# An encoder trunk with expert retrieval: gather indices copied on VectorE, sparse steps from the fourth tile, smaller last dumps

## The chip, the cores and the metric

The kernel runs on one core of one Trainium2 chip. The metric is the device time of one execution in microseconds (us). Three runs of the kernel before took 1835.06 us in the median, 1828.98 at the least and 1835.87 at the most. The engines are called TensorE (PE, with PEld for its weight loads), VectorE (DVE), ScalarE (ACT), GpSimd (POOL) and SyncE (SP). SP here only issues the loads of weights; POOL issues the gathers.

## The reference

Two layers over 272 tokens (256 and 16 meta tokens) of width 1024. Layer 0 mixes tokens with a recurrent block, layer 1 with a convolution; behind each mixer stands the same retrieval of experts (PEER):

```
q = (xc @ w_query)                             # 8 heads, two halves
s1, i1 = top_k(scores[:, :, 0], 16); s2, i2 = top_k(scores[:, :, 1], 16)
cand = s1[..., :, None] + s2[..., None, :];  s, flat = top_k(cand, 16)
expert = idx1 * 128 + idx2                     # one of 16384 experts
g = softmax(s)
act = gelu(einsum('chkd,cd->chk', expert_u[expert], xc))
out = einsum('chk,chkd->cd', g * act, expert_v[expert])
```

Each token and head picks 16 of 16384 experts; an expert's row of U gives an activation, its row of V is added with that weight. Everything is float32.

## The kernel before

**Dense passes.** For most tokens the kernel does not gather experts. It multiplies all of them: the *U pass* computes the activations of all 128 x 128 experts for a block of tokens, one tile of 128 experts after another, weighs them by a one-hot product (`g_unit`), and the *V pass* multiplies them by all rows of V, again in 128 tiles. A tile of weights is loaded by SP into one of four buffers `raw` (`load`), split into a high and a low part (`load_split`, L137: `hi` on ScalarE L144, `lo` on VectorE or POOL L151) and multiplied. In the V pass a tile is eight products with `hi` (L718) and eight with `lo` (L722), which add up in PSUM. The activations are split the same way, four tiles at a time (`weights`, L260 and L263).

**Few tokens.** Tokens that don't fit the dense block are served sparsely, in groups of 16 tokens, where a partition is one head of one token. A group is *early*, *late* or *drawn*. In layer 1 one group is early (from token 240) and two are drawn (224 and 208); in layer 0 one is early, one late, none drawn. For early and late groups, rows of U are gathered by POOL (`few_rows`, L989) and multiplied on VectorE (`few_dot`, L998). A drawn group's activations exist already, as its tokens went through the dense U pass. They are dumped to a table in DRAM, and each of its 16 activations a partition is then fetched by one gather of one number a partition (`few_draw`, L1004). For all groups, rows of V are gathered by POOL and added up on VectorE (`few_add`, L1027 and L1029), with two rows asked for ahead.

**Dumps.** `few_dump` copies a piece of the activations to a tile `own` (L698, two buffers) and sends it to the table (L699), both on POOL. Before the change a piece is 32 of 128 rows; four pieces for each of two groups, the last ones behind the last tile of the U pass. The list `dumps` says behind which tile of the second half of U a piece goes.

**The order of the V pass.** `few_plan` makes a list of steps (load of `wide`, dots, activation, weighing, adds) and spreads them over the tiles of V: a step has a tile at which it is due. Draws get due tiles of their own, a dozen tiles or more into the pass. `few_step` runs behind each tile: it takes one piece of the pending top-k work (`picks`, the generator `few_late`: per drawn group nine pieces, then a softmax), then all steps that are due:

```
        with self.tc.issue_after(self.dve_lo.ins):
            while self.picks:
```

The block around it ties VectorE's instructions of this tile behind the tile's `lo`; instructions on other engines in the block are not tied. What runs when on POOL and SP is decided by a planner that orders the program by its own costs, by data and by buffers. The scratch of the picks and the rows lies in pools that are opened when the pool of `own` is closed.

Of the kernel before, what the change touches and what calls it, by code (L numbers as in the profile page):

```python
# [7 lines left out]
F32 = mybir.dt.float32  # L8
F32R = mybir.dt.float32r
F16 = mybir.dt.float16  # L10
U32 = mybir.dt.uint32
# [6 lines left out]
P = 128  # L18
# [6 lines left out]
TOPK = 16  # L25
NK = 128
# [7 lines left out]
FEW = META  # L34
# [2 lines left out]
DOTS_FROM, DOTS, AHEAD, LO_FROM = 48, 10, 2, 41  # L37
JG = 4
JA = 64
JD = 32  # L40
FULL = (("v", 1024),)
SQ_AT = 4
PE_TAPS = (0, 0, 0, 0, 0, 6, 31, 31)
# [18 lines left out]
class Trunk:  # L62
# [481 lines left out]
    def peer(self, layer, n, xs):  # L544
        tc, nc, a = self.tc, self.nc, self.a
# [9 lines left out]
        with tc.tile_pool(name=f"few{layer}", bufs=1) as kp:  # L555
# [3 lines left out]
            act_a = ap0.tile([P, JA, nu], F32, name="act_a")  # L559

            with tc.tile_pool(name=f"top{layer}", bufs=1) as sp:
# [7 lines left out]
                early, late = [], []  # L569
# [22 lines left out]
                drawn = [self.few_pick(sp, kp, q, xs, layer, t0) for t0 in DRAWN[layer]]  # L592
# [31 lines left out]
            with tc.tile_pool(name=f"act1{layer}", bufs=1) as ap1:  # L624
                act_b = ap1.tile([P, NK - JA, nu], F32, name="act_b")
# [3 lines left out]
                rp = drawn_pool.__enter__()  # L629
                dumps = {}  # L630
                for g, few in enumerate(drawn):
                    few["table"] = self.dp.tile([P, NK, FEW], F32, name=f"own{layer}_{few['t0']}")
                    for j in range(0, NK, JD):
                        dumps.setdefault(j + JD - 1 - JA if j >= JA else (g * JA + j) // JD * 8 + 3, []).append((few, j))

                def weigh(dst, g):
                    nc.vector.scalar_tensor_tensor(dst, g, scale, dst, op0=OP.mult, op1=OP.mult)  # L637
# [23 lines left out]
                def g_unit(c0, jd):  # L661
                    cs = slice(c0, c0 + CC)
                    one_hot(c0)
                    ps = self.px.tile([P, CC, NK], F32, tag=f"g{c0 // CC % 2}", name="g")
                    for c in range(CC):
                        A, Bh, Bl = hot.pop(c0 + c)
                        nc.tensor.matmul(ps[:, c, :], A, Bh, start=True, stop=False)  # L667
                        nc.tensor.matmul(ps[:, c, :], A, Bl, start=False, stop=True)  # L668
                    pj = ps.rearrange("p c j -> p j c")
                    weigh(act_a[:, :, cs], pj[:, :JA, :])  # L670
                    if jd > JA:
                        weigh(act_b[:, :jd - JA, cs], pj[:, JA:jd, :])
                    if jd < NK:
                        nc.scalar.activation(act_b[:, jd - JA:, cs], pj[:, jd:, :], AF.Copy, scale=scale)  # L674
# [4 lines left out]
                def u_out(i, ps):  # L679
                    cd = at[0] * CC  # L680
                    w = act_b[:, i, :]
                    if cd < nu:
                        nc.scalar.activation(w[:, cd:], ps[:, cd:], AF.Gelu_apprx_tanh)
                    if cd > 0:
                        tmp = hp.tile([P, n], F32, tag="tmp", name="tmp")
                        nc.scalar.activation(tmp[:, :cd], ps[:, :cd], AF.Gelu_apprx_tanh)
                        nc.vector.tensor_tensor(w[:, :cd], w[:, :cd], tmp[:, :cd], op=OP.mult)
                    for few, j in dumps.get(i, ()):
                        few_dump(few, j)
                    upto = min(len(chunks), (i + 1) * len(chunks) // (NK - JA - 4))  # L690
                    for c0 in chunks[at[0]:upto]:
                        g_unit(c0, JA + i + 1)
                    at[0] = upto

                def few_dump(few, j):
                    own = rp.tile([P, JD, FEW], F32, tag="own", name="own")
                    act, o = (act_a, j) if j < JA else (act_b, j - JA)
                    nc.gpsimd.tensor_copy(own, act[:, o:o + JD, few["t0"]:few["t0"] + FEW])  # L698
                    nc.gpsimd.dma_start(few["table"][:, j:j + JD], own)  # L699

                acc = []
                self.upper(f"gate{layer}")
                self.linears([U[j] for j in range(JA, NK)], xs, nu, (("v", 1024),), u_out)
                hot_pool.__exit__(None, None, None)
                drawn_pool.__exit__(None, None, None)
# [3 lines left out]
                vp = row_pool.__enter__()  # L709
# [291 lines left out]
            few["rows"][nxt] = self.few_rows(pool, few, self.a["u_rows"], 0, nxt, ahead + 1)  # L1001

    def few_draw(self, few, k):
        self.nc.gpsimd.indirect_dma_start(  # L1004
            out=few["act"][:, k:k + 1], out_offset=None, in_=few["table"].rearrange("p j (t o) -> (p j t) o", o=1),
            in_offset=bass.IndirectOffsetOnAxis(ap=few["ids"][:, 0, k:k + 1], axis=0))

    def few_gelu(self, few, last):
        self.nc.scalar.activation(few["act"], few["act"], AF.Gelu_apprx_tanh)
# [23 lines left out]
    def few_plan(self, vp, kp, early, late, drawn, scale, layer, ahead=2):  # L1033
        steps = []
        draws = []
        for few in early + late + drawn:
            lo = DOTS if few in early else 0
            if few["drawn"]:
                draws += [(len(steps), lambda few=few, k=k: self.few_draw(few, k)) for k in range(TOPK)]
            else:  # L1040
                steps += [lambda few=few: self.few_load(vp, few)]
                steps += [lambda few=few, lo=lo, k=k: self.few_dot(vp, few, k, lo, TOPK, ahead) for k in range(TOPK - lo + ahead)]
                steps += [lambda few=few: self.few_gelu(few, few is (early + late)[-1])]
            steps += [lambda few=few: self.few_weigh(few, scale)]
            steps += [lambda few=few, k=k: self.few_add(vp, few, k, ahead) for k in range(TOPK + ahead)] + [few]
        self.steps = [(1 + i * (NK - 4 * JG - 1) // len(steps), f) for i, f in enumerate(steps)]
        first = 12 * (len(late) + 1)
        for i, (at, f) in enumerate(draws):
            g, k = divmod(i, TOPK)
            lo, hi = first + 12 * g, self.steps[at][0] - 3  # L1050
            draws[i] = lo + k * (hi - lo) // TOPK, f
        self.steps = sorted(self.steps + draws, key=lambda s: s[0])
        self.sums = []
        self.picks = [self.few_late(kp, few, layer) for few in late + drawn]

    def few_step(self, j):
        with self.tc.issue_after(self.dve_lo.ins):
            while self.picks:
                try:
                    next(self.picks[0])  # L1060
                    break
                except StopIteration:
                    self.picks.pop(0)
            while self.steps and self.steps[0][0] <= j:
                f = self.steps.pop(0)[1]
                if callable(f):
                    f()
                else:
                    self.sums.append((j + 4, f))
        while self.sums and self.sums[0][0] <= j:  # L1070
            yield self.sums.pop(0)[1]
# [245 lines left out]
```

## Time and profile before

| what | before |
|---|---|
| median of three runs | 1835.06 us |
| the profiled execution, its own time | 1841.34 us |
| its span | 1839.5 us |
| TensorE busy (share of the span) | 1770.1 us (96%) |
| VectorE busy | 1508.1 us (82%) |
| ScalarE busy | 914.6 us (50%) |
| POOL busy | 473.8 us (26%) |
| mean DMA rate | 215 GB/s |

The span is the time from the first to the last instruction of the program in the profile. Times of rows are counted from its start. A row of a timeline has start, duration, engine, line, operation, tiles and shape, and in brackets how long the engine had been idle and what released it; `remote` and "another core or an unknown queue" stand for a releaser that the profile cannot name. Layer 1's U pass runs to about 1468 us, its V pass from there to the end.

### The profile page before, as it was taken

The numbers are of one execution on the slowest core, as the hardware profiler recorded it, in microseconds if no ns is written. First come the engines' busy times: TensorE is split into PE (matmuls) and PEld (weight loads), VectorE is DVE, ScalarE is ACT, GpSimd is POOL, SyncE is SP. The second block draws the span as 40 slices with busy tenths as digits, with TensorE's granted clock in tenths as the row PEclk, the third lists the DMA queues.
The fourth block names the chain that finished last, engine by engine and source line by source line (L and its number), as shares of the span: only waits on it lengthen the run. The fifth ranks groups of instructions, "written<-read, shape, count | busy, mean of one in ns | idle before, by whom it ended". The sixth has DMA issues, their size and how long they took to land.

```text
span 1839.5 us, 35003 instructions
## 1 busy us (share of the span) xinstructions
PE 1770.1 (96%) x13500; PEld 1691.4 (92%) x13500; DVE 1508.1 (82%) x2863; ACT 914.6 (50%) x1510; POOL 473.8 (26%) x308
## 2 busy tenths in 40 slices
PE   8999999999999999999998999999999976999996
PEld 7899999999998999999887999999999976999996
DVE  7786996989998877786799869969889884878775
ACT  6544444554444546875432554445544433445452
POOL 1102992000002223130000029922000055423310
PEclk9999999999999999999999999999999997999998
DMA  5446667655558888897440455677555565989883
GB/s 196 160 162 161 197 195 259 233 163 170 167 170 299 303 299 284 291 320 239 151 148 24 156 166 184 197 259 256 172 181 174 164 241 177 337 306 348 297 285 127
DMA packets 111896, 396.22 MB, mean 215 GB/s; under 512 B 13296, under 2 KB 14448, under 8 KB 111600
## 3 DMA queue, kind: packets, MB, share of 16 engines
q1 hardware_dynamic: 91632, 324.74, 53.0%
q0 software_dynamic: 20096, 69.23, 10.5%
q8 instruction: 106, 1.74, 0.4%
q14 instruction: 62, 0.51, 0.1%
HBM read 387.04 MB, written 6.88 MB: 214 GB/s over the span
## 4 chain that ended last, share of the span: by engine, by line
PE 82%; DVE 10%; DMA 2%; issue 2%; POOL 2%; ACT 1%; another core or an unknown queue 1%; POOLq 0%; SPq 0%; DVEq 0%; ACTq 0%
PE u L179 41%; PE acc L718 21%; PE acc L722 12%; PE u L215 3%; DVE cy L1197 2%; DVE odd L1197 2%; PE g L667 1%; PE g L668 1%; DVE lo L151 1%; DMA raw<-peer_v 1%; POOL lo L151 1%; PE sps L576 1%; PE acc L757 0%; PE pre L235 0%
## 5 line engine op out<-in xcount | busy, mean ns | idle before, releaser
L144 ACT ACTIVATE hi<-raw 128x1024 fp32r<-128x1024 f32 x556 | 588.1, 1059 | 651.0 <-PE u L179 211.6
L151 DVE TENSOR_TENSOR lo<-raw,hi 128x1024 fp32r<-128x1024 f32 x474 | 579.5, 1226 | 194.2 <-PE u L179 66.8
L179 PE MATMUL u<-xs,hi 128*128 128x240 f32 (+2 forms) x4544 | 569.4, 277 | 0.6 <-DVE xs L378 0.6
L179 PEld LDWEIGHTS u<-xs,hi 128*128 128x128 f32 x4544 | 537.6, 189 | 1.4 <-DVE xs L378 1.0
L718 PE MATMUL acc<-w,hi 128*128 128x480 f32 (+1 forms) x1984 | 451.3, 370 | 2.8 <-DVE w L263 1.9
L718 PEld LDWEIGHTS acc<-w,hi 128*128 128x128 f32 x1984 | 358.3, 191 | 27.3 <-DVE w L263 2.3
L179 PE MATMUL u<-xs,lo 128*128 128x240 f32 (+2 forms) x2272 | 308.0, 276 | 5.8 <-POOL lo L151 3.7
L722 PEld LDWEIGHTS acc<-w,lo 128*128 128x128 f32 x2048 | 270.7, 193 | 40.4 <-DVE lo L151 20.7
L722 PE MATMUL acc<-w,lo 128*128 128x240 f32 (+1 forms) x2048 | 276.1, 277 | 27.0 <-DVE lo L151 17.3
L179 PEld LDWEIGHTS u<-xs,lo 128*128 128x128 f32 x2272 | 280.6, 189 | 7.7 <-POOL lo L151 4.6
L151 POOL TENSOR_TENSOR lo<-raw,hi 128x1024 fp32r<-128x1024 f32 x82 | 211.6, 2596 | 106.0 <-ACT hi L144 84.1
L989 POOL DMA_INDIRECT rows<-peer_v,ids x80 | 126.5, 1581 | 262.9 <-DVE few_out L1029 154.4
L989 POOL DMA_INDIRECT rows<-u_rows,ids x48 | 60.4, 1259 | 402.1 <-DVE sv L870 222.7
L215 PE MATMUL u<-x,raw 128*128 128x272 f32 x480 | 114.2, 398 | 5.1 <-DMA x<-h 5.1
L215 PEld LDWEIGHTS u<-x,raw 128*128 128x128 f32 x480 | 92.6, 193 | 24.5 <-DMA raw<-w_in 5.1
L1029 DVE SCALAR_TENSOR_TENSOR few_out<-rows,act,few_out 128x1024 f32<-128x1024 f32 x75 | 95.9, 1279 | 0.9 <-DMA rows<-peer_v,ids 0.5
L674 ACT ACTIVATE act_b<-g 128x432 f32<-128x432 f32 (+41 forms) x56 | 21.9, 390 | 107.9 <-DVE act_b L637 91.8
L650 DVE TENSOR_TENSOR AB<-iota,iT 128x2048 f16<-128x2048 f16 x56 | 68.1, 1220 | 0.1
L998 DVE SCALAR_TENSOR_TENSOR rows<-rows,wide 128x1024 f32<-128x1024 f32 x48 | 58.5, 1218 | 0.0
L667 PE MATMUL g<-AB 128*128 128x128 f16 x448 | 56.6, 220 | 0.0
L668 PE MATMUL g<-Bl,AB 128*128 128x128 f16 x448 | 56.0, 219 | 0.0
L263 DVE TENSOR_TENSOR w<-act_b,w 128x960 fp32r<-128x960 f32 (+1 forms) x32 | 34.9, 1090 | 24.3 <-ACT w L260 24.1
(279 smaller groups left out, 1771.5 us busy)
## 6 DMA issues: line engine op xcount, KB each, us to landing
raw<-peer_u SPq DMA_DIRECT2D x256, 512.0 KB
raw<-peer_v SPq DMA_DIRECT2D x248, 512.0 KB
raw<-w_query SPq DMA_DIRECT2D x28, 512.0 KB
raw<-pw SPq DMA_DIRECT2D x22, 512.0 KB
raw<-w_in SPq DMA_DIRECT2D x16, 512.0 KB
raw<-w_out SPq DMA_DIRECT2D x8, 512.0 KB
raw<-peer_v SPq DMA_DIRECT2D x16, 256.0 KB
wide<-wide SPq DMA_DIRECT2D x5, 512.0 KB
```

What stands on the lines that cost most here:

```text
L144: self.act_hi = nc.scalar.activation(hi, raw, AF.Copy).ins
L151: i = e.tensor_tensor(lo[:, s], raw[:, s], hi[:, s].bitcast(F32), op=OP.subtract)
L179: self.mm = nc.tensor.matmul(ps[:, :n], l[:, k, :], xs(k, r)[:, :n], start=start, stop=stop)
L215: self.mm = self.nc.tensor.matmul(ps[:, :n], raw[:, k, :], x[:, k, :n], start=k == 0, stop=k == NB - 1)
L650: nc.vector.tensor_tensor(AB.rearrange("p x c (a b) -> p (x c) a b", b=2), keys, iT[:, c0 // HC].rearrange("p x c b -> p (x c) b")[:, :, N ...
L667: nc.tensor.matmul(ps[:, c, :], A, Bh, start=True, stop=False)
L668: nc.tensor.matmul(ps[:, c, :], A, Bl, start=False, stop=True)
L718: self.mm = nc.tensor.matmul(acc[b][:, :2 * n].rearrange("p (a t) -> p a t", a=2), hi, w[:, :, :n], start=j == 0, stop=j == NK - JG - 1, s ...
L722: self.mm = nc.tensor.matmul(main[b][:, :n], hi if p_ else lo, w[:, i, :n], start=False, stop=j == NK - 1 and not p_, skip_group_check=True)
L989: self.nc.gpsimd.indirect_dma_start(out=t, out_offset=None, in_=table, in_offset=bass.IndirectOffsetOnAxis(ap=few["ids"][:, i, k:k + 1], a ...
L1029: nc.vector.scalar_tensor_tensor(few["out"], t, w, few["out"], op0=OP.mult, op1=OP.add)
L1197: nc.vector.scalar_tensor_tensor(z, h, w, z, op0=OP.mult, op1=OP.add)
```

## The change

Four edits. Pieces of a dump have the borders 0, 32, 64, 96, 120 and 128, so there are five for each group, and the last one has 8 rows. `few_draw` first copies its column of indices on VectorE, from `ids` to a new tile `turn`, and the gather reads the copy; VectorE's copy falls under the tie behind the `lo` of its tile. In a layer with drawn groups, the steps are spread from tile 4 on (before: from tile 1) over 108 in place of 111 tiles, and the first draws are due at tiles 15 and 27 (before: 12 and 24). The picks start behind tile 3 (before: tile 0).

```diff
-JD = 32
+PIECES = (0, 32, 64, 96, 120, 128)
...
-                    for j in range(0, NK, JD):
-                        dumps.setdefault(j + JD - 1 - JA if j >= JA else (g * JA + j) // JD * 8 + 3, []).append((few, j))
+                    for i, j, j1 in zip(range(NK), PIECES, PIECES[1:]):
+                        dumps.setdefault(j1 - 1 - JA if j >= JA else 16 * g + 8 * i + 3, []).append((few, j, j1))
...
-                def few_dump(few, j):
-                    own = rp.tile([P, JD, FEW], F32, tag="own", name="own")
-                    act, o = (act_a, j) if j < JA else (act_b, j - JA)
-                    nc.gpsimd.tensor_copy(own, act[:, o:o + JD, few["t0"]:few["t0"] + FEW])
-                    nc.gpsimd.dma_start(few["table"][:, j:j + JD], own)
+                def few_dump(few, j, j1):
+                    own = rp.tile([P, 32, FEW], F32, tag="own", name="own")[:, :j1 - j]
+                    act, o = (act_a, 0) if j < JA else (act_b, JA)
+                    nc.gpsimd.tensor_copy(own, act[:, j - o:j1 - o, few["t0"]:few["t0"] + FEW])
+                    nc.gpsimd.dma_start(few["table"][:, j:j1], own)
...
     def few_draw(self, few, k):
+        self.nc.vector.tensor_copy(few["turn"][:, k:k + 1], few["ids"][:, 0, k:k + 1])
         self.nc.gpsimd.indirect_dma_start(
             out=few["act"][:, k:k + 1], out_offset=None, in_=few["table"].rearrange("p j (t o) -> (p j t) o", o=1),
-            in_offset=bass.IndirectOffsetOnAxis(ap=few["ids"][:, 0, k:k + 1], axis=0))
+            in_offset=bass.IndirectOffsetOnAxis(ap=few["turn"][:, k:k + 1], axis=0))
...
             if few["drawn"]:
+                few["turn"] = vp.tile([P, TOPK], U32, name=f"turn{few['t0']}")
...
-        self.steps = [(1 + i * (NK - 4 * JG - 1) // len(steps), f) for i, f in enumerate(steps)]
-        first = 12 * (len(late) + 1)
+        begin = 4 if drawn else 1
+        self.steps = [(begin + i * (NK - 4 * JG - begin) // len(steps), f) for i, f in enumerate(steps)]
+        first = begin + 11 * (len(late) + 1)
...
         self.picks = [self.few_late(kp, few, layer) for few in late + drawn]
+        self.picks_at = begin - 1
...
-            while self.picks:
+            while self.picks and j >= self.picks_at:
```

More of the change, by code (lines that the diff above doesn't have):

```diff
@@ L687, in u_out @@
                         nc.vector.tensor_tensor(w[:, :cd], w[:, :cd], tmp[:, :cd], op=OP.mult)
-                    for few, j in dumps.get(i, ()):
-                        few_dump(few, j)
+                    for piece in dumps.get(i, ()):
+                        few_dump(*piece)
                     upto = min(len(chunks), (i + 1) * len(chunks) // (NK - JA - 4))
```

## The prediction

> **What bounds the kernel now.** I read the page first, then the chain of waits in order of time, then a table of engine busy time by stretches, then the timelines of the engines around each hole.
>
> ```profile
> span 1839.5 us, 35003 instructions
> ...
> PE 82%; DVE 10%; DMA 2%; issue 2%; POOL 2%; ACT 1%; another core or an unknown queue 1%; POOLq 0%; SPq 0%; DVEq 0%; ACTq 0%
> ```
>
> TensorE carries 82% of the chain that ended last, so a change pays only where TensorE stands idle. All edits act in layer 1: with no drawn group (layer 0) the first step stays at 1 and the picks at 0, and no dump exists. So layer 0, and layer 1 up to its V pass but for two more dumps, should not move. The chain shows where layer 1's V pass is not TensorE's:
>
> ```profile
> 1468.67 2.35 POOL own L698 x2
> ...
> 1530.93 5.40 another core or an unknown queue
> 1537.64 11.43 another core or an unknown queue
> ```
>
> Two places: one behind the last dumps of `own` at 1468, one at 1530 to 1549 whose releaser the profile cannot name. The table of stretches sizes them (us; columns PE, PEld, DVE, ACT, POOL busy, granted clock, DMA share, GB/s):
>
> ```profile
> core 0: us, PE busy (x) PEld busy (x) DVE busy (x) ACT busy (x) POOL busy (x), PEclk, DMA share, GB/s
> 1486.00:1503.00 17.00, 16.82 (x106) 16.32 (x105) 16.82 (x42) 9.00 (x10) 8.37 (x7) 0.96 0.84 314
> 1503.00:1526.00 23.00, 19.90 (x127) 18.49 (x127) 19.34 (x43) 10.84 (x13) 18.12 (x17) 1.00 0.63 206
> 1526.00:1551.00 25.00, 10.53 (x38) 8.99 (x36) 5.92 (x14) 5.36 (x7) 15.51 (x16) 0.62 0.30 106
> 1551.00:1615.00 64.00, 64.00 (x413) 63.43 (x413) 54.55 (x49) 30.77 (x32) 27.36 (x16) 0.96 0.92 327
> ```
>
> From 1551 on TensorE is full, with POOL at 27.36 of 64 us. From 1526 to 1551 nearly everything is idle but POOL (15.51 of 25 us): TensorE 10.53, VectorE 5.92, the DMA engines 0.30. The tiles of V are counted on TensorE's timeline by the starts of the eight `hi` products (L718):
>
> ```profile
> 1475.50 1.68 PE L718 MATMUL acc<-w,hi 128*128 128x416 f32 x8
> ...
> 1488.91 1.68 PE L718 MATMUL acc<-w,hi 128*128 128x416 f32 x8
> ...
> 1491.31 1.69 PE L718 MATMUL acc<-w,hi 128*128 128x416 f32 x8
> ...
> 1500.91 1.69 PE L718 MATMUL acc<-w,hi 128*128 128x416 f32 x8
> ...
> 1519.88 1.69 PE L718 MATMUL acc<-w,hi 128*128 128x416 f32 x8
> ...
> 1524.69 1.69 PE L718 MATMUL acc<-w,hi 128*128 128x416 f32 x8
> ...
> 1556.30 1.68 PE L718 MATMUL acc<-w,hi 128*128 128x416 f32 x8
> ```
>
> A free tile takes 1491.31 - 1488.91 = 2.40 us. **Hole 1**: 1475.50 to 1488.91 is 13.41 us for two tiles, so 8.6 are lost. **Middle**: 1500.91 to 1519.88 is 18.97 for six tiles, 4.5 lost. **Hole 2**: 1524.69 to 1556.30 is 31.61 for four tiles, 22.0 lost (the last 1.6 of it while the clock comes back from the 0.62 of the table).
>
> **Hole 1, part by part.** First what stands in it on POOL, VectorE and SP's queue:
>
> ```profile
> 1468.67 2.35 POOL L698 COPY own<-act_b 128x512 f32<-128x512 f32 x2 [96.65 <-ACT act_b L683]
> 1470.97 1.07 POOL L699 DMA_DIRECT2D own<-own  x2
> ```
> ```profile
> 1478.36 0.49 DVE L870 MAX8 sv<-sc 128x8 f32<-128x128 f32 x2 [5.05 <-issue]
> ...
> 1482.55 1.21 DVE L151 TENSOR_TENSOR lo<-raw,hi 128x1024 fp32r<-128x1024 f32 x1
> ```
> ```profile
> SPq L1015 <- DMA own<-own: 7.2, 1, 7.2
> ```
>
> The last U tile ends, POOL copies two pieces of 512 numbers a partition (2.35) and sends them (1.07). The top-k scratch of the sparse part lies where `own` was, so VectorE's first MAX8 waits 5.05 us, and SP's load of `wide` waits 7.2 us with the next loads of V queued behind it. Then VectorE works 4.2 us on top-k (1478.36 to 1482.55) ahead of the `lo` that TensorE needs.
>
> The change moves the first pick behind the fourth `lo` and the first step, with the load of `wide`, to tile 4; in between TensorE gets `lo` for tile 3 without a sparse instruction ahead of it. The last piece has 8 rows, not 32. Its two copies cost between a quarter of 2.35 (0.6) and all of it, so the DMAs are out at 1470.3 to 1472.0. How long they need to land is bounded by nothing and by the 6.2 us of before (1472.04, when issued, to 1478.2, when the queue moved): 1470.3 to 1478.2. I take 1474, as data shrinks fourfold but some of those 6.2 us is not data. The first pick now follows the `lo` of tile 3, which can end at about 1474.5, so VectorE does not wait; SP may wait a little, and four buffers of V (9.6 us) stand ahead of TensorE. Hole 1 goes, with a rest of 0 to 3 us; I take 1.
>
> Here the Trainium skill speaks against the smaller piece: its page "DMA: Bandwidth & Descriptors", section "Anatomy of one DMA — SWDGE (gpsimd) path", gives a transfer that POOL issues about 2.0 us plus one for every 436 KB, so 256 KB would take 2.6 and 64 KB 2.15 us (estimates). By it the cut in size saves 0.45 us of landing, and only the earlier issue and the later steps would pay; the sum would keep its term for hole 1, as the later steps alone clear it. The trace's 6.2 us for 256 KB is far over the rule, so the rest is a wait that no size explains.
>
> The 4.2 us of top-k that ran inside the hole now run beside tiles. VectorE has 2.40 - 1.21 (`lo`) - 0.25 (a quarter of the 1.02 us split of weights, below) = 0.9 us a tile; six tiles take them all. Bounds 0 to 4.2, I take 1.
>
> ```profile
> 1489.15 1.02 DVE L263 TENSOR_TENSOR w<-act_a,w 128x832 fp32r<-128x832 f32 x1
> ```
>
> **The middle stays.** VectorE was busy 16.82 of 17 us up to 1503. There the second group's top-k, the first one's softmax and six dot products ask for more than 0.9 us a tile. All are moved by the same three tiles, so they meet again: 4.5 us lost before and after, between 3 and 6; no gain.
>
> **Hole 2.** POOL and VectorE:
>
> ```profile
> L1004 POOL DMA_INDIRECT act<-own,ids x32: 943/948/1946, 1496.7 to 1545.1; - x32
> ```
> ```profile
> 1525.63 0.95 POOL L1004 DMA_INDIRECT act<-own,ids  x1 [0.30 <-issue]
> ...
> 1545.14 0.94 POOL L1004 DMA_INDIRECT act<-own,ids  x1 [0.30 <-issue]
> ```
> ```profile
> 1530.89 0.18 DVE L985 COPY z<-z 128x16 f32<-128x16 f32 x1
> ...
> 1549.15 2.36 DVE L151 TENSOR_TENSOR lo<-raw,hi 128x1024 fp32r<-128x1024 f32 x2 [11.51 <-remote]
> ```
>
> The 32 one-number gathers ("draws") wait for nothing but their indices, so POOL fires them as fast as it can: the last 16 start 1.25 to 1.3 us apart, from 1525.63 to 1545.14. The hole begins with this burst and ends 3 us behind it. In it the longest wait of a `lo` is 11.51 us, for a mark of another unit although the products before it had long been issued. While draws mix with row gathers and VectorE is the limit (1503 to 1526: 17 POOL instructions, 18.12 us) TensorE loses little; it is the pure burst that kills. What it holds up I can't name; that it is the burst is inference from the two edges and from POOL being alone at work.
>
> After the change each draw needs a one-column copy on VectorE that is pinned behind the `lo` of its tile. By the plan the first group draws at tiles 15, 17, ... 45, the second at 27, 30, ... 74: one in 4.8 us, then about one in 3, then one in 7. The burst is gone, and with it 22.0 us. Added: 32 copies of one number a partition, at most 0.18 each (16 numbers): 5.8 us if all lie bare, nothing where VectorE has room (54.55 of 64 busy); two or three fall into the middle. I take 0.5. On POOL a draw now waits for its copy with row gathers queued behind it: in tiles 27 to 45 there are 0.8 draws and 0.65 row gathers a tile, 1.45 x 1.71 (27.36/16) = 2.5 us by the slow rate of the full stretch, 1.45 x 1.3 = 1.9 by the burst's period, against 2.40. POOL is close to full there. Price between 0 and 19 tiles x 0.1 + a doubled draw's hold-up at three tiles, 2 to 5 us; I take 1, nearer the burst's period.
>
> The two extra dumps at tile 55 of the second half of U are two POOL copies under 2.35 us together, beside a TensorE that POOL does not feed there (splits are VectorE's): nothing; uncovered, 2.35. Steps keep their count and spread over 108, not 111, tiles: nothing.
>
> **Sum.** -8.6 - 22.0 + 1 + 1 + 0.5 + 1 = -27.1 us. The profiled execution took 1841.34 us (its span is 1839.5), 6.3 over the median 1835.06 of runs from 1828.98 to 1835.87. It becomes 1814.2; the median 1835.06 - 27.1 = **1808**.
>
> **Rivals.** (1) *Draws spaced out still hold things up.* For it: I know the cause only by its edges. Against: 16 draws among row gathers, before 1525, cost next to nothing. Then hole 1 alone goes: 1835 - 8.6 + 1.5 = 1828, with half of hole 2 1817.
>
> (2) *Hole 1 stays*, because the planner sends `wide` to SP where it did before, its buffer being free early, and the dump still lands late. For: SP's queue isn't tied to the tile, only VectorE's work is. Against: picks are tied. 1808 + 8.6 = 1817.
>
> (3) *Slower.* A draw at POOL's head waits for VectorE's copy; the row gather behind it comes late; VectorE's in-order queue stops at the add of that row with the next `lo` behind it, and TensorE stops. Place: tiles 15 to 74, where draws and adds meet. It decides once a row is issued less than about a tile before its add. Price: a tile, 2.40 us, for each draw so hit; 12 hits pay back the whole gain, and 16 (half the draws) give 1808 + 38 = 1846. Against: rows are asked for two steps (3 tiles, 7 us) ahead, and before the change adds hardly waited for rows:
>
> ```profile
> L1029 DVE SCALAR_TENSOR_TENSOR few_out<-rows,act,few_out 128x1024 f32<-128x1024 f32 x75 | 95.9, 1279 | 0.9 <-DMA rows<-peer_v,ids 0.5
> ```
>
> (4) *The change doesn't bite*: copies end up together on VectorE and the burst stays. Against: each is pinned behind its own tile's `lo`. This is rival (1)'s 1828.
>
> **Chances.** What can be told from no change is 0.5%, 9.2 us, so faster means under 1825.9 and slower over 1844.2. Likeliest case 0.67 (its own range 1800 to 1816: all extra costs zero and a run as far under the median as 1828.98 was, to the upper bounds of picks and POOL); rival 2 0.08; rivals 1 and 4 0.17, half of it under 1825.9; rival 3 0.08. Faster 0.67 + 0.08 + 0.07 = 0.82, same 0.10, slower 0.08. The range goes from 1799 to 1829, through rivals 1 and 2, and leaves rival 3 out.
>
> **What would show it.** Right: no MAX8 wait over 1 us at the start of V; SP's `wide` behind more loads of V; draws one by one with a wait on VectorE's copy, none closer than 2 us for long; TensorE over 95% in all of V; about 4.5 us still lost in tiles 12 to 18. Wrong: an unnamed releaser of `lo` over 3 us near draws (rival 1), adds waiting for rows (rival 3), SP waiting on `own` over 3 us (rival 2).

## The result and the profile after

| | before | after |
|---|---|---|
| median of seven runs | 1835.06 us (1828.98 to 1840.95) | 1821.79 us (1818.46 to 1824.83) |
| ratio, with its 95% interval | | 0.9929 (0.9909 to 0.9948) |
| the profiled execution | 1841.34 us | 1818.46 us |

The change makes the kernel 13.3 us (0.7%) faster. The forecast was 27.1 us: the side is right, the time lies in the range, the size is twice what came. Medians, ratios and intervals here and below leave out five executions that took 2734 to 4578 us. The two profiled executions differ by 22.9 us, because the one before lay 6.3 us over its median and the one after 3.3 us under. Whoever compares only these two sees almost the forecast; the medians don't.

The page of the changed kernel: span, busy time of each engine, and the shares of the chain that ended last.

```profile
span 1816.7 us, 35056 instructions
...
PE 1764.0 (97%) x13500; PEld 1688.1 (93%) x13500; DVE 1512.8 (83%) x2895; ACT 913.8 (50%) x1510; POOL 475.9 (26%) x312
...
PE 67%; DVE 8%; DMA 2%; ACT 1%; issue 1%; POOL 1%; POOLq 0%; DVEq 0%; ACTq 0%; SPq 0%
```

TensorE's share of the span went from 96% to 97%, and "another core or an unknown queue" is gone from the chain. The table of stretches (columns as in the prediction) shows the three places:

```profile
core 0: us, PE busy (x) PEld busy (x) DVE busy (x) ACT busy (x) POOL busy (x), PEclk, DMA share, GB/s
1476.00:1489.00 13.00, 10.64 (x72) 10.25 (x71) 10.98 (x34) 4.84 (x5) 3.83 (x3) 1.00 0.84 325
...
1503.00:1516.00 13.00, 9.79 (x52) 8.64 (x51) 12.73 (x40) 5.35 (x6) 2.45 (x3) 0.87 0.77 252
...
1534.00:1590.00 56.00, 56.00 (x376) 55.76 (x375) 51.75 (x64) 27.98 (x29) 39.70 (x32) 1.00 0.96 343
```

From 1534 to 1590, where hole 2 was, TensorE is full with POOL busy for 39.70 of 56 us. Hole 1 is smaller, not gone (10.64 of 13). The middle is as empty as before or emptier: 9.79 of 13, while VectorE works 12.73. TensorE's timeline, by the start of the eight `hi` products of a tile (the rows of `lo` between them are left out), gives the same in tiles:

```profile
1483.64 1.69 PE L718 MATMUL acc<-w,hi 128*128 128x416 f32 x8
1488.68 1.68 PE L718 MATMUL acc<-w,hi 128*128 128x416 f32 x8
...
1503.08 1.69 PE L718 MATMUL acc<-w,hi 128*128 128x416 f32 x8
1506.53 1.69 PE L718 MATMUL acc<-w,hi 128*128 128x416 f32 x8
1511.67 2.65 PE L718 MATMUL acc<-w,hi 128*128 128x416 f32 x8
1515.89 1.68 PE L718 MATMUL acc<-w,hi 128*128 128x416 f32 x8
```

Against 2.40 a tile, hole 1 loses 1488.68 - 1483.64 - 2.40 = 2.6 us, and three tiles of the middle lose 12.81 - 7.2 = 5.6; two later tiles make it 7.2. In the table of experiments "lost" is the sum of such excesses from about 1470 to 1788; it holds some 5 us that every kernel has, such as the tiles in which a group's finished sum is multiplied in. Before it was 44.6, after 20.4. Ahead of the V pass nothing moved: its first product starts at 1468.2 before and at 1469.2 after.

What is left of hole 1 shows on SP's queue, POOL, VectorE, ScalarE and the DMA issues, one row each:

```profile
SPq L1016 <- DMA own<-own: 4.1, 1, 4.1
```
```profile
1469.64 1.70 POOL L698 COPY own<-act_b 128x128 f32<-128x128 f32 x2 [22.61 <-ACT act_b L683]
1471.29 1.07 POOL L699 DMA_DIRECT2D own<-own  x2
```
```profile
1476.10 0.30 DVE L870 MAX8 sv<-sc 128x8 f32<-128x128 f32 x1 [0.58 <-DMA own<-own]
```
```profile
1481.37 1.06 ACT L144 ACTIVATE hi<-raw 128x1024 fp32r<-128x1024 f32 x1 [4.49 <-DMA raw<-peer_v]
```
```profile
own<-own POOLq DMA_DIRECT2D x2, 64.0 KB, 4.0
```

A quarter of the data took 0.85 us a copy where the large piece took 1.17, and 4.0 us from issue to landing, where the large pieces of a second profile of before (*again*, below) took 6.0. VectorE's wait is down from 5.05 to 0.58 us. SP's is not gone (it loads `wide` and `xr` besides the weights): `wide` still waits 4.1 us (7.2 before) at the head of the queue, then brings its 512 KB ahead of the next loads of V, and ScalarE waits 4.49 us for one of them. By the Trainium skill ("DMA: Bandwidth & Descriptors", section "Anatomy of one DMA — SWDGE (gpsimd) path") 64 KB take about 2.15 us (an estimate from its formula); the trace has 4.0, and the two sizes differ by 2.0 us, not by the 0.45 that the prediction worked out from it.

Hole 2's copies and draws cost what was put down for them or less: the adds wait little for their rows (groups of instructions, whole span).

```profile
L1030 DVE SCALAR_TENSOR_TENSOR few_out<-rows,act,few_out 128x1024 f32<-128x1024 f32 x75 | 96.1, 1281 | 1.3 <-DMA rows<-peer_v,ids 1.3
```

### The profile page after: what moved, and what is told of

Its sections match the earlier page's. It is cut to its first block, busy times and chain, and to the rows that moved or that the text cites. A ratio compares the mean times of both kernels' runs of the same rounds, so it can differ in the third digit from the quotient of the medians.

```text
span 1816.7 us, 35056 instructions
## 1 busy us (share of the span) xinstructions
PE 1764.0 (97%) x13500; PEld 1688.1 (93%) x13500; DVE 1512.8 (83%) x2895; ACT 913.8 (50%) x1510; POOL 475.9 (26%) x312
## 4 chain that ended last, share of the span: by engine, by line
PE 67%; DVE 8%; DMA 2%; ACT 1%; issue 1%; POOL 1%; POOLq 0%; DVEq 0%; ACTq 0%; SPq 0%
PE u L179 30%; PE acc L718 20%; PE acc L722 12%; DVE cy L1201 2%; DVE odd L1201 2%; DMA raw<-peer_v 1%; PE g L667 1%; PE g L668 1%; DVE lo L151 1%; POOL lo L151 1%; ACT hi L144 1%; DMA rows<-u_rows,ids 0%; PE acc L757 0%; PE pre L235 0%; PE sps L576 0%
## 5 line engine op out<-in xcount | busy, mean ns | idle before, releaser
L989 POOL DMA_INDIRECT rows<-peer_v,ids x80 | 120.7, 1509 | 215.5 <-DVE few_out L1030 98.9
L698 POOL COPY own<-act_b 128x512 f32<-128x512 f32 (+2 forms) x6 | 5.4, 934 | 190.1 <-ACT act_b L683 190.1
```

Source lines behind the costliest of these rows:

```text
L989: self.nc.gpsimd.indirect_dma_start(out=t, out_offset=None, in_=table, in_offset=bass.IndirectOffsetOnAxis(ap=few["ids"][:, i, k:k + 1], a ...
```

## The experiments

Four sets of kernels, each timed beside the kernel before on one chip. The differences come from the ratios, at 1834 us; medians of different sets are not to be subtracted from one another. "Lost" is of one profiled execution each, and it was the fastest of its kernel for the change, *pieces_only*, *tied_after* and *copy9*, the slowest for *after_again* and *tied*.

| kernel | median | against before (95%) | lost in V |
|---|---|---|---|
| again: before, unchanged | 1834.86 | +0.4 (-2.4 to +3.1) | 39.1 |
| turn_only: index copies alone | 1822.86 | -11.0 (-13.2 to -8.6) | 23.3 |
| no_turn: the change without copies | 1829.26 | -5.0 (-6.8 to -3.1) | 32.7 |
| no_draws: before, draws left out | 1820.05 | -14.1 (-16.3 to -11.7) | 21.9 |
| after_again: the change once more | 1822.07 | -13.6 (-16.5 to -10.6) | 25.1 |
| tied: before, draws ordered behind rows | 1822.66 | -12.7 (-15.6 to -9.9) | 29.5 |
| busy: two POOL copies for a draw | 1822.04 | -11.6 (-14.3 to -8.6) | 25.2 |
| busy4: four POOL copies for a draw | 1830.95 | -2.9 (-5.3 to -0.6) | 33.2 |
| tied_after: change, tied for copies | 1820.74 | -11.9 (-15.0 to -8.8) | 19.3 |
| pieces_only: smaller pieces alone | 1831.30 | -0.9 (-2.9 to +1.1) | 28.7 |
| shift_only: later steps and picks alone | 1839.13 | +3.9 (+1.3 to +6.4) | 41.1 |
| wide9: change, `wide` later on SP | 1818.67 | -15.0 (-18.7 to -11.6) | 20.3 |
| copy9: wide9, `xr` later, longer spread | 1812.52 | -19.8 (-23.3 to -16.5) | 14.5 |
| best9: copy9, tied for copies | 1818.33 | -16.5 (-20.4 to -12.8) | 20.9 |

### Is hole 2 there every time, and what makes it?

Theory A: the burst of draws makes hole 2 in every execution, of varying length, and the profiled one of before was long. Theory B: hole 2 was one bad execution, and the gain is hole 1's. *again* is the kernel before; *turn_only* has the first hunk below alone; *no_turn* is the changed kernel without it; *no_draws* replaces the 32 gathers by one constant, so that the output of the drawn groups' 32 tokens is not the reference's.

```diff
 def few_draw(self, few, k):
+    self.nc.vector.tensor_copy(few["turn"][:, k:k + 1], few["ids"][:, 0, k:k + 1])
...
-            in_offset=bass.IndirectOffsetOnAxis(ap=few["ids"][:, 0, k:k + 1], axis=0))
+            in_offset=bass.IndirectOffsetOnAxis(ap=few["turn"][:, k:k + 1], axis=0))
```
```diff
 def few_draw(self, few, k):      # no_draws
-    self.nc.gpsimd.indirect_dma_start(
...
+    if k == 0:
+        self.nc.vector.memset(few["act"], 0.5)
```

> The kernel before, unchanged, for a second trace and its scatter. Theory A (the burst of unpaced draws makes hole 2 in every execution, but of changing length, and the profiled execution before, 1841.34 us, had a long one): ratio 1.00, and the new trace has a hole behind the last draws of 8 to 22 us. Theory B (hole 2 was one bad execution, and the gain of 13 us comes from hole 1): no hole over 5 us there.

> Only the copies of the indices on VectorE; steps from tile 1 and old pieces stay. Theory A: hole 2 goes, hole 1 (8.6 us) stays: 10 to 18 us faster than before, and TensorE loses under 2 us where the draws end. Theory B: no change, within 3 us of before.

> The change without the copies: steps from tile 4 and small last pieces, draws read their indices directly. Theory A: hole 1 shrinks to about 3 us, hole 2 stays: 3 to 8 us faster than before. Theory B: the whole 13 us.

> The kernel before with its 32 draws left out (the activations of the drawn groups are a constant instead, so the output of 32 tokens is not the reference's). The ceiling of what the draws cost. Theory A: as turn_only or up to 3 us better, with no hole at the place of the draws. Theory B: within 3 us of before. If the draws cost something beyond their burst, it is over 5 us better than turn_only.

Measured: the copies alone bring 11.0 us, the rest alone 5.0, and leaving the draws out 14.1. B falls. One number missed: hole 1 lost 6.9 us in *no_turn*, not about 3. But the second profile of before (1835.54 us, near the median) shows a hole of another kind. Timelines of POOL, VectorE and TensorE in *again*:

```profile
1527.43 0.95 POOL L1004 DMA_INDIRECT act<-own,ids  x1 [0.31 <-DVE z L934]
...
1550.96 0.94 POOL L1004 DMA_INDIRECT act<-own,ids  x1 [0.30 <-issue]
1552.21 0.94 POOL L989 DMA_INDIRECT rows<-peer_v,ids  x1 [0.30 <-issue]
```
```profile
1542.37 1.22 DVE L151 TENSOR_TENSOR lo<-raw,hi 128x1024 fp32r<-128x1024 f32 x1
1556.66 1.29 DVE L1029 SCALAR_TENSOR_TENSOR few_out<-rows,act,few_out 128x1024 f32<-128x1024 f32 x1 [13.07 <-DMA rows<-peer_v,ids]
1557.87 1.22 DVE L151 TENSOR_TENSOR lo<-raw,hi 128x1024 fp32r<-128x1024 f32 x1
```
```profile
1546.98 1.68 PE L718 MATMUL acc<-w,hi 128*128 128x416 f32 x8
1559.14 2.03 PE L722 MATMUL acc<-w,lo 128*128 128x208 f32 x8 [10.48 <-DVE lo L151]
```

POOL issues sixteen draws in a row, from 1527.43 to 1551.9, and only then the row gather that stands behind them in its order. VectorE is ready for that row's add at 1543.6 and waits 13.07 us; the next `lo` stands behind the add, and TensorE, which had `hi` products left, waits 10.48 us for it. The hole is 13.1 us with its aftermath, not 22.0, and nothing in it has an unnamed releaser. *no_turn* has the same, 11.69 us:

```profile
1559.87 1.28 DVE L1029 SCALAR_TENSOR_TENSOR few_out<-rows,act,few_out 128x1024 f32<-128x1024 f32 x1 [11.69 <-DMA rows<-peer_v,ids]
```

So a new pair of theories. Q: the hole is POOL's own order, a row gather behind sixteen draws. D: the burst of one-number gathers does it as traffic, or the copies matter in themselves.

### Q against D

*tied* keeps before's 32 draws and adds no copy; each draw is only ordered behind the last row gather (`row_ins`) that stands before it in the text. *busy* and *busy4* take the draws out (a constant in their place, as in no_draws) and keep POOL busy with two or four copies for each.

```diff
 def few_draw(self, few, k):      # tied
+    with self.tc.issue_after(self.row_ins.ins):
         self.nc.gpsimd.indirect_dma_start(
```
```diff
 def few_draw(self, few, k):      # busy; busy4 has range(4)
-    self.nc.gpsimd.indirect_dma_start(
...
+    if k == 0:
+        self.nc.vector.memset(few["act"], 0.5)
+    for i in range(2):
+        self.nc.gpsimd.tensor_copy(self.idle[i % 2], few["ids"][:, 0])
```

> The changed kernel once more, for a second profile beside the same runs of the kernel before as the three kernels below. Expected by both theories: 11 to 15 us under the kernel before, two executions apart in the stretch of hole 1 by up to 4 us, no add of the sparse groups waiting more than 1.5 us for its row.

> The kernel before, without index copies, with each draw ordered on POOL behind the last row gather that stands before it in the text. Same 32 draws, same indices, nothing added on VectorE. Theory Q (hole 2 is a row gather that stands behind sixteen draws in POOL's own order, and the add that waits for it, with the next lo behind it): the hole goes as it did with the copies, the longest wait of an add for its row is under 2 us, and the time falls by 11 to 14 us, since the copies' 32 x 0.14 us are not there. Theory D (what delays the others is the burst of one-number gathers as traffic, or the copies matter in themselves): with one to three draws at a time the traffic is spread too, so a gain would not speak against D; but if the copies themselves matter, the time stays within 3 us of before.

> The kernel before with no draws: in the place of each, POOL makes two copies of the 128x16 indices to a scratch tile, and the activations of the two drawn groups are a constant, so the output of their 32 tokens is not the reference's. POOL is kept busy as in the burst (2 copies at 0.75 to 0.9 us for a draw at 1.25 to 1.5), with no DMA of a draw. Theory Q: one add waits 8 to 18 us for its row as in the kernel before, the V pass loses 35 to 45 us, and the time is within 5 us of the kernel before. Theory D: without the gathers nothing is held up, no add waits over 1.5 us, the time is 12 to 16 us under the kernel before, as it was with the draws left out.

> The changed kernel with the later steps and the smaller pieces, but no index copies: each draw is ordered on POOL behind the last row gather before it, as in the kernel named tied. Theory Q: as fast as the changed kernel or up to 4 us faster, as 32 copies leave VectorE, where the middle of the V pass is short of time (7 us lost in tiles 12 to 18). If the copies matter in themselves: back to the time of the kernel without them, 5 us under the kernel before.

> The kernel named busy with four copies of the indices in the place of a draw, not two: at the measured 0.39 us a copy the block of the second group lasts 16 x 4 x 0.39 = 25 us, as the 24.8 us of the sixteen draws. The draws are left out, the activations of the drawn groups are a constant. Theory Q: the fourth row for the adds of the first group is issued at about 1550, as with the draws, the add waits 10 to 16 us for it, the V pass loses 35 to 42 us, and the time is within 4 us of the kernel before. If what a row gather waits behind did not decide, it would stay as busy (5.0 us for that add, 24 us lost in the V pass, 11 us under the kernel before).

Measured for *busy*: a miss of mine first. A copy took 0.39 us, not 0.75 to 0.9, so the block lasted 19.3 us, and the add waited 4.96, under Q's 8 to 18 and over D's 1.5. Its timelines of POOL and VectorE:

```profile
1520.63 19.31 POOL L1007 COPY idle<-ids 128x16 uint32<-128x16 uint32 x50 [4.02 <-DVE ids L973]
1540.10 1.83 POOL L989 DMA_INDIRECT rows<-peer_v,ids  x1 [0.15 <-DVE act L1005]
```
```profile
1548.45 1.28 DVE L1030 SCALAR_TENSOR_TENSOR few_out<-rows,act,few_out 128x1024 f32<-128x1024 f32 x1 [4.96 <-DMA rows<-peer_v,ids]
```

The time, 11.6 us under before, lay just outside D's 12 to 16 and far from Q's 5 at most. A shorter block can explain that, or Q is wrong, so *busy4* doubled the dose:

```profile
1525.23 29.18 POOL L1007 COPY idle<-ids 128x16 uint32<-128x16 uint32 x100 [4.02 <-DVE ids L973]
1554.95 0.96 POOL L989 DMA_INDIRECT rows<-peer_v,ids  x1 [0.54 <-issue]
```
```profile
1559.42 1.28 DVE L1030 SCALAR_TENSOR_TENSOR few_out<-rows,act,few_out 128x1024 f32<-128x1024 f32 x1 [10.14 <-DMA rows<-peer_v,ids]
```

With no draw at all, a busy POOL brings back the hole (the add waits 10.14 us) and 8.7 of the 11.6 us that *busy* had gained. (The block was 29 us long, not 25, and the loss 33.2 fell short of the 35 to 42 expected.) With all 32 draws and no copies, *tied* brings 12.7 us, as much as the copies do. Q holds: what counted was what the row gather stands behind. Traffic of single gathers is not needed for it (*busy4* has none); that it adds something is not ruled out. The copies act by putting the draws in VectorE's order, one per due tile. *tied* also shows the rest of the mechanism in small; up to three draws still stand between two rows, and here one took 4.10 us, so that an add waited 5.67, not under 2 as expected (POOL, then VectorE):

```profile
1581.12 4.10 POOL L1005 DMA_INDIRECT act<-own,ids  x1 [0.30 <-issue]
1585.53 2.03 POOL L1005 DMA_INDIRECT act<-own,ids  x1 [0.30 <-issue]
1587.87 2.02 POOL L989 DMA_INDIRECT rows<-peer_v,ids  x1 [0.30 <-issue]
```
```profile
1596.73 1.29 DVE L1030 SCALAR_TENSOR_TENSOR few_out<-rows,act,few_out 128x1024 f32<-128x1024 f32 x1 [5.67 <-DMA rows<-peer_v,ids]
```

*tied_after* is as fast as the change within the intervals; its hoped-for 4 us did not show. *after_again* repeats the size of the change, 13.6 us, and loses 8.4 us in hole 1 where the first profile lost 2.6, more than the 4 us apart that were expected: that hole varies. ScalarE's wait for a load of V behind `wide` is 7.64 us here, where it was 4.49:

```profile
1486.65 1.06 ACT L144 ACTIVATE hi<-raw 128x1024 fp32r<-128x1024 f32 x1 [7.64 <-DMA raw<-peer_v]
```

### Hole 1: smaller pieces, later steps, and `wide`

*pieces_only* and *shift_only* take the other two parts of the change alone (the hunks of `dumps` and `few_dump`; those of `few_plan` and `few_step`). *wide9* is the changed kernel with the load of `wide` due at tile 9 and ordered behind that tile's load of V (`raw_ins`; the line that keeps it is left out):

```diff
-    def few_load(self, pool, few, tag="wide", bufs=2):
+    def few_load(self, pool, few, tag="wide", bufs=2, behind=False):
...
-        self.nc.sync.dma_start(few["x"], few["kept"].rearrange("h t d -> (h t) d"))
+        with self.tc.issue_after(self.raw_ins.ins) if behind else nullcontext():
+            self.nc.sync.dma_start(few["x"], few["kept"].rearrange("h t d -> (h t) d"))
...
-        begin = 4 if drawn else 1
-        self.steps = [(begin + i * (NK - 4 * JG - begin) // len(steps), f) for i, f in enumerate(steps)]
+        begin, steps_at = (4, 9) if drawn else (1, 1)
+        self.steps = [(steps_at + i * (NK - 4 * JG - steps_at) // len(steps), f) for i, f in enumerate(steps)]
```

> The kernel before with the smaller last pieces of the dumps alone: steps, picks and draws as before, no copies. Theory: of the 4.9 us that the change brought without its index copies, the smaller piece makes the part by which SP waits less for own (7.1 down to about 4): 2 to 3.5 us, hole 1 loses 5.5 to 7.5 us; hole 2 stays (an add waits 10 to 16 us). Rival (the later picks made it all): within 1 us of the kernel before.

> The kernel before with the later steps and picks alone (first step at tile 4, picks behind tile 3, draws due at 15 and 27): the four pieces of a dump and the draws as before, no copies. If the later steps and picks made the gain of hole 1: 3 to 5 us under the kernel before, no MAX8 waits over 1 us, hole 1 loses 4 to 7 us with SP still waiting about 7 us for own. If smaller pieces and later steps pay only together (SP's wait of 7 us for the large last piece keeps the hole open whatever VectorE does): within 1.5 us of the kernel before, hole 1 loses 8 to 10 us. Hole 2 stays in both (an add waits 10 to 16 us).

> The changed kernel with one more edit for hole 1: the load of wide is due at tile 9 and ordered on SP behind the load of the tenth tile of V (it stands behind the sixth in both kernels); the other steps follow it from tile 9 on, the picks stay at tile 3. Theory W (what is left of hole 1 in the changed kernel is wide at the head of SP's queue, waiting 4.1 us for the last dump, and then its 512 KB beside the late loads of V): SP's wait for own is under 0.5 us, hole 1 loses under 2 us in each execution where the changed kernel lost 2.6 and 8.4 in its two, the middle loses less too, as dots and picks overlap for fewer tiles; 3 to 7 us under the changed kernel. Rival (the picks on VectorE or the gathers of U rows keep hole 1 open): SP's wait goes, the loss in tiles 4 to 10 stays at 2 to 8 us, and the time stays within 2 us of the changed kernel.

Measured: the pieces alone are worth 0.9 us, not told from nothing, although SP's wait fell from about 7 to 4.2 us and hole 1 to 5.8 us in the profile, both as expected. The later steps alone cost 3.9 us, which neither expectation had. Added up they would be 3.0 us slower; together (*no_turn*) they are 5.0 us faster. So the two parts pay only together. The likely reason, by the waits below: with the large last piece VectorE still waits for it, even three tiles later, and with the small one alone the picks still stand in front of the first `lo` and wait too. VectorE's first MAX8 in *shift_only* and in *pieces_only*:

```profile
1481.54 0.29 DVE L870 MAX8 sv<-sc 128x8 f32<-128x128 f32 x1 [3.65 <-DMA own<-own]
```
```profile
1476.60 0.49 DVE L870 MAX8 sv<-sc 128x8 f32<-128x128 f32 x2 [3.64 <-DMA own<-own]
```

The 8.4 us that *shift_only* loses in hole 1 are the second expectation's. Its hole 2 is smaller than expected (an add waits 6.2 us, 7.7 us lost). The middle loses 13.7 us in tiles 14 to 19, where *again* loses 4.6, and there ScalarE waits for a releaser without a name while the first group's draws run:

```profile
1519.77 1.06 ACT L144 ACTIVATE hi<-raw 128x1024 fp32r<-128x1024 f32 x1 [5.18 <-remote]
1526.94 1.06 ACT L144 ACTIVATE hi<-raw 128x1024 fp32r<-128x1024 f32 x1 [6.10 <-remote]
```

That is the sign of the profiled execution of before, in another kernel with bursts; it comes back below. The profile took 1842.89 us, 3.8 over its kernel's median, so how much of the 3.9 us it explains is not shown.

*wide9*: SP no longer waits for `own` in this stretch, hole 1 loses 1.2 us, and the time is 1.4 to 2 us under the change by the ratios, with overlapping intervals. For hole 1 theory W holds: *copy9* and *best9*, which keep this edit, lose 1.1 and 1.3 us there, where the four profiles of the change and its variants with `wide` at its old place lose 2.6, 8.4, 6.9 and 2.6. W's 3 to 7 us of time did not come. The middle, which was to lose less, lost 9.8 us in the profile, against 7.2 after the change.

### A version that beats both

*copy9* adds two edits to wide9: `xr`, 1 MB for the end, is ordered on SP behind the 120th load of V, and the steps spread to tile 116. *best9* is copy9 with `tied` in place of the copies.

```diff
-                        for i in range(2):
-                            nc.sync.dma_start(xr[:, 4 * i:4 * i + 4, :], ...)
+                        with tc.issue_after(self.raw_ins.ins) if layer else nullcontext():
+                            for i in range(2):
+                                nc.sync.dma_start(xr[:, 4 * i:4 * i + 4, :], ...)
...
-(NK - 4 * JG - steps_at)
+((NK - 3 * JG if drawn else NK - 4 * JG) - steps_at)
```

> wide9 with two more edits: the 1 MB of xr is ordered on SP behind the 120th load of V (it stands behind the 62nd), and the steps spread over four tiles more, up to tile 116. Expected: the 2 to 4 us lost at tiles 61 and 62 go, so 2 to 4 us under wide9; if the load of xr only moves the same loss to the last tiles, no gain against wide9.

> copy9 without the index copies: each draw is ordered on POOL behind the last row gather before it, as in the kernel named tied. 32 copies (0.14 us each, 4.6 us) leave VectorE. If VectorE's time in the middle still limits: 1 to 4 us under copy9 (1812.5); if POOL's order limits (up to four draws between two row gathers, one of them of 4.1 us in the kernel tied): 1 to 5 us over it, with an add that waits over 2 us.

*copy9* takes 1812.52 us, ratio 0.9892 (0.9873 to 0.9910): by the ratios 6 to 7 us under the changed kernel, and 5 under wide9 (6 by the medians of their set), more than expected. Its page and two of its stretches:

```profile
span 1808.8 us, 35055 instructions
```
```profile
1503.00:1516.00 13.00, 10.85 (x68) 9.51 (x66) 12.83 (x31) 4.82 (x6) 4.62 (x5) 1.00 0.70 222
...
1590.00:1665.00 75.00, 74.76 (x500) 74.05 (x499) 61.09 (x64) 36.88 (x38) 38.37 (x27) 1.00 0.90 318
```

From 1590 to 1665, where `xr` was loaded, TensorE is busy 74.76 of 75 us. The middle is now the largest hole, about 5 us, with VectorE at 12.83 of 13. How much of this is the spread and how much `xr` was not taken apart. *best9* is 3 us over copy9 by the ratios and 6 by the medians, with overlapping intervals, as the second expectation had it. Its longest wait of an add, 2.16 us, stands behind a slow stretch of POOL, a draw of 3.17 us and then two rows of about 3 us each (POOL, VectorE):

```profile
1652.95 3.17 POOL L1006 DMA_INDIRECT act<-own,ids  x1 [0.30 <-issue]
1656.42 2.95 POOL L990 DMA_INDIRECT rows<-peer_v,ids  x1 [0.30 <-issue]
1659.68 3.17 POOL L990 DMA_INDIRECT rows<-peer_v,ids  x1 [0.30 <-issue]
```
```profile
1664.19 1.29 DVE L1032 SCALAR_TENSOR_TENSOR few_out<-rows,act,few_out 128x1024 f32<-128x1024 f32 x1 [2.16 <-DMA rows<-peer_v,ids]
```

That the copies are worth their 4.6 us on VectorE, because a draw that waits for its tile keeps POOL free for rows, is likely here and not shown: the rows themselves were slow, and *tied_after* was no slower than the change.

## Why the prediction was right or wrong

**Where** was right: all of the gain is in layer 1's V pass, in hole 2 and hole 1, and TensorE sets the time. In the sum, -22.0 + 0.5 + 1 for hole 2 became -11.0 (*turn_only*), and -8.6 + 1 + 1 for hole 1 became -2.3 more (13.3 less 11.0; the same edits without the copies bring -5.0, *no_turn*).

**Hole 2, the step that failed.** "The burst is gone, and with it 22.0 us": the term was measured on one execution 6.3 us over the median, and then taken from the median. The second profile of before has 13.1 in its place; with the draws left out altogether the gain is 14.1, so 22.0 was never to be had. The cause was off too. That it is the burst is right, but what it held up, in the four ordinary profiles with bursts or POOL copies as long (*again*, *no_turn*, *pieces_only*, *busy4*: an add waits 10 to 13 us), was a row gather in POOL's own order. That is rival 3's chain (row gather late, add waits, `lo` behind it), which I put on the side of a loss: it was what before already suffered from. I ruled it out by the row in which the adds wait 0.9 us in all; that row, too, is of the unusual execution, whose 22.0 us are another mechanism (the last paragraph of this section). The same group in *again*:

```profile
L1029 DVE SCALAR_TENSOR_TENSOR few_out<-rows,act,few_out 128x1024 f32<-128x1024 f32 x75 | 96.0, 1280 | 14.5 <-DMA rows<-peer_v,ids 14.5
```

**Hole 1.** "Hole 1 goes, with a rest of 0 to 3 us; I take 1." The picks did as said: 0.58 us of wait where at most 1 was forecast. The load of `wide` did not: it stands behind the sixth load of V in both kernels and waited 4.1 us, against the 3 that were named as the sign of rival 2. The rest was 2.6 in one execution and 8.4 in another. That "the later steps alone clear it" was wrong as well: *shift_only* loses 8.4 us there. Rival 2 was half true and had a chance of 0.08. (A slip in the chances beside it: half of 0.17 is 0.085, and the sum takes 0.07.)

**The middle.** "No gain" is right, "stays" is not: 7.2 us in the first profile of the change and 5.7 in the second, for 4.5. VectorE is at 12.73 of 13 us, so work that leaves hole 1, and the copies, probably come due here; no run takes them apart. The sum had 1 us for top-k that moves beside tiles.

**Copies and POOL.** A copy took 0.14 us (0.18 was the bound), POOL's share of the full stretch rose from 43% to 71%, and the adds wait 1.3 us in all: nothing speaks against 0.5 and 1. Rivals 1 and 4 didn't come: with copies no wait of `lo` has an unnamed releaser.

**What stays open.** In the profiled execution of before and in *shift_only* marks came late, by an unnamed releaser, up to 11.51 and 6.10 us. The traces say whose marks. Each of these waits ends within 0.1 us of a mark by which TensorE tells that products are done, while the products had ended long before: the mark at 1549.07 in before comes 6.7 us behind TensorE's last product, the one at 1526.86 in *shift_only* 6.5 us. In the V pass of the other fourteen profiles no such mark is more than 0.5 us late. The same two traces are short of records where the draws run: between 1500 and 1560 us before holds 211 marks of landed DMAs and *shift_only* 346, while *again*, with the instructions of before, holds 924. So what delayed the marks may belong to the taking of the profile; no run tells (the trace of *best9* lacks some 500 such marks as well, without a late one of TensorE). All late marks stand in kernels that fire draws in bursts; none of the five profiles with index copies and none of the three without draws shows them, but *again*, *no_turn* and *pieces_only* have bursts and don't show them either. That bursts cause it is not shown.

## What to carry to other kernels

Before costing an add's wait, write down the issuing engine's own order: a gather that is early by its data can stand behind sixteen others, and the consumer's in-order engine then stops work that has nothing to do with it. A cheap dependence that releases each gather at its tile was as good here as an explicit order. A hole from one profile is subtracted from that profile's own time; if that lies over the median, take a second profile before the hole becomes a term. Here a second one changed the size of the hole and its cause.

## What the runs showed of the hardware

The time for which a one-number gather kept POOL varied from 0.94 to 4.10 us in the same kernel (*tied*), and a run of sixteen took 24.5 us in *again*. A write of 64 KB to the table landed 3.9 to 4.1 us after its issue in six profiles and one of 256 KB 6.0 to 6.8 us in six others: a quarter of the bytes took about six tenths of the time. And two executions of one kernel can differ in their mechanism, not only in length: before lost 22.0 us with marks that came late in one, and 13.1 us by POOL's order in another.
